# Splitting the first load of b by contraction slice in a GELU matmul chain

## The chip, the cores and the metric

The kernel runs on one core of one Trainium2 chip. The metric is the device time of one execution in microseconds (us), as the median of several runs. Engines are named as the profile names them: PE is TensorE (matmuls; PEld its weight loads), DVE is VectorE, ACT is ScalarE, POOL is GpSimd, SP is SyncE, which here only issues DMAs.

## What is computed

```python
# a: 1024 x 1024, b: 1024 x 2048, c: 2048 x 1024, all float32
h = a @ b
h = gelu_tanh(h)          # 0.5*h*(1 + tanh(sqrt(2/pi)*(h + 0.044715*h**3)))
out = (h @ c).astype(float32)   # 1024 x 1024
```

## The kernel before

The whole order of work is written out by hand (`tc.manual_schedule()`, line 33): each engine runs its instructions in the order of the source, and waits between engines are made from the tiles that they write and read. The matmuls take bfloat16 operands in the first stage and mixed ones later.

**The main body.** The first product is made transposed: tile `hT[h]` holds gelu of a block of 128 columns of `b` by 512 rows of `a`. Columns 0 to 511 of `b` are multiplied plainly (`mm1`, line 112, by `block`, line 156), in eight contraction slices of 128 rows each (k = 0 to 7) and two halves of `a`'s rows (h = 0, 1). The other columns of `b`, and after them the second product with `c`, go through `seven` (line 306), a scheme with seven block products in place of eight (sums of blocks on DVE, products on PE, line 212). Stores of the result are issued by SP as the second product's blocks come out (`done2`, line 431, and `store`, line 428).

**The start, which the change touches.** `a` comes with rows on the partitions and has to be turned, so its path is: DMA to `sta` (float32), cast to bfloat16 `ab` (`cast_a`, line 128, the copies themselves at lines 108 for ACT and 110 for DVE), transposes on PE through a PSUM tile `pt` (`turn`, line 138, the transposes at line 145), copy to `aT` on DVE (line 146). `b` needs only a cast from `stb` to `b1` (`cast_b`, line 149).

SP issues five loads, lines 75 to 79, one behind the other on one queue:

| line | what it loads | size | read by |
|---|---|---|---|
| 75 | `a`, first 512 rows, columns 0 to 255, to `sta` | 512 KB | `cast_a(0, 0)` on DVE |
| 76 | `b`, contraction slices 0 and 1, columns 0 to 511, to `stb[:, 0:2]` | 512 KB | `cast_b(0)` on DVE and ACT, `cast_b(1)` on ACT |
| 77 | `a`, last 512 rows, columns 0 to 255 | 512 KB | `cast_a(1, 0)` on DVE and ACT |
| 78 | `a`, first 512 rows, columns 256 to 511 | 512 KB | `cast_a(0, 1)` on ACT and DVE |
| 79 | `b`, slice 2, columns 0 to 511 | 256 KB | `cast_b(2)` on ACT |

All other loads are issued by POOL on its own queue and cast on the way (lines 85 to 104). POOL holds them back with one small copy, `gate` (line 81), that waits for line 75's data.

Until the first data is there, PE runs filler matmuls on a constant (`stir`, line 122, recorded at line 125). The order around the first matmuls is, on all engines together:

```python
stir(256, 256, 256, 256, 256)
tn = turn(0, 0, 4, cast_a(0, 0, nc.vector))
next(tn)                                     # 4 transposes, copy to aT (slice 0)
stir(128)
cast_b(0, nc.vector, nc.vector, nc.scalar)   # 128 + 128 columns on DVE, 256 on ACT
next(tn)                                     # 4 transposes, copy to aT (slice 1)
stir(64)
cast_b(1, nc.scalar)                         # 512 columns on ACT
ab = cast_a(1, 0, nc.vector, nc.scalar)      # needs line 77's data
block(0, range(4), (0,))                     # 4 matmuls of slice 0
block(0, range(2), (1,))                     # 2 matmuls of slice 1
for _ in turn(1, 0, (7, 6), ab):             # 8 transposes of line 77's data
    pass
```

**The stores.** SP's queue has eight completion semaphores, which its transfers take in turn; a transfer waits, when it is issued, for the one eight places before it. Before the change SP issues 5 loads and 19 stores, 24 in all. In `done2` the blocks (i, l) = (0, 0) with j = 1 and j = 2 are stored in two halves each, as the first results of the second product; the ones that follow are stored whole, up to the last two, which are halves again (line 376).

Of the kernel before, what the change touches and what calls it, by code (L numbers as in the profile page):

```python
# [19 lines left out]
def kernel(ctx, tc, a, b, c, out):  # L20
    nc = tc.nc
# [3 lines left out]
    H = 512  # L25
# [4 lines left out]
    bv = b.rearrange("(kt p) n -> p kt n", p=128)  # L30
# [9 lines left out]
    def slot(tag, shape, dt, name):  # L40
        return big.tile(shape, dt, name=name, tag=tag)
# [4 lines left out]
    def pieces(tag, bufs, shape, dt, name):  # L46
        return small.tile(shape, dt, name=name, tag=tag, bufs=bufs)
# [17 lines left out]
    stb = slot("x0", [128, KT, H], F32, "stb")  # L65
# [3 lines left out]
    def a_part(h, q):  # L69
        return av[:, 4 * h:4 * h + 4, ds(q * 256, 256)]  # L70

    def b_part(q):
        return bv[:, 2 * q:2 * q + 2, 0:H]

    nc.sync.dma_start(out=sta[:, 0, 0], in_=a_part(0, 0))  # L75
    nc.sync.dma_start(out=stb[:, 0:2], in_=b_part(0))  # L76
    nc.sync.dma_start(out=sta[:, 1, 0], in_=a_part(1, 0))
    nc.sync.dma_start(out=sta[:, 0, 1], in_=a_part(0, 1))
    nc.sync.dma_start(out=stb[:, 2], in_=bv[:, 2, 0:H])
# [19 lines left out]
    for n in range(2):  # L99
        for k in range(0, KT, 4):  # L100
            nc.gpsimd.dma_start(out=b2[:, k:k + 4, ts(n, H)],
                                in_=bv[:, k:k + 4, ds(1024 + n * H, H)])
# [151 lines left out]
    for q in range(1, 3):  # L254
        k = 2 * q
# [172 lines left out]
    def store(mt, q0, w, ot, eng=None):  # L428
        (eng or nc.sync).dma_start(out=out[ts(mt, 128), ds(q0, w)], in_=ot)

    def done2(i, l, j, p):
        if (i, l) == (1, 0):
            ot = pieces("o", 4, [128, H], F32, "ot")
            nc.vector.tensor_copy(ot, p)
            p = ot
        n = 2 if (i, l) == (0, 0) and j else 1
        for q in range(n):
            r = ds(q * (H // n), H // n)
            store(4 * i + j, l * H + q * (H // n), H // n, p[:, r])

    def between2(n):
# [12 lines left out]
        elif n == "P73":  # L454
            two.t4(two.t[1], 4)

    seven(two, done2, between2)


# [28 lines left out]
```

## Time and profile before

| | us |
|---|---|
| median of 3 runs (117.45 to 117.9) | 117.73 |
| span of the profiled execution, first to last instruction | 115.7 |
| median less span | 2.0 |
| PE busy in that span | 111.1 (96%) |
| DVE busy | 90.0 (78%) |
| ACT busy | 51.4 (44%) |
| granted TensorE clock, mean | 1.00 |

The profiled execution has no time of its own beside its span; the table sets the span against the median of the timed runs. All times below count from the first instruction of the profiled execution. An engine's busy time is the union of its instructions; TensorE's instructions overlap each other, so that a matmul of 512 columns is recorded with 0.379 us while matmuls in a row start every 0.216 us. "Landing" is the time at which the last of a DMA's completion events arrived; each of the 16 DMA engines sends one.

The chain of work that ended last is PE for 90% of the span and DMA for 5%. 21 MB are read from HBM; the DMA engines are busy until about 54 us, after that only with stores.

### The profile page before, as it was taken

To read this page: it belongs to the slowest core of one execution; us is meant where nothing else is said; L and a number is where in the kernel's file an instruction comes from. 1 tells how busy PE (TensorE), PEld (TensorE's weight loads), DVE (VectorE), ACT (ScalarE), POOL (GpSimd) and SP (SyncE) were. 2 spreads that over 40 slices of the span, in tenths; PEclk is the share of its full clock that TensorE was granted. 3 is DMA by queue.
4 is the path that set the end of the run, shared out by engine and by line. 5 is a ranking of instruction groups with operands and counts; after the bars stand their busy time and mean duration, and the time that the engine had idled before them with its cause. 6 is when DMAs were issued, how large, how long until landed. Compare 5 with 4: busy or idle time off the path is not lost.

```text
span 115.7 us, 1461 instructions
## 1 busy us (share of the span) xinstructions
PE 111.1 (96%) x542; PEld 77.1 (67%) x542; DVE 90.0 (78%) x107; ACT 51.4 (44%) x86; POOL 17.2 (15%) x29
## 2 busy tenths in 40 slices
PE   7989999999999999999999999999999999999980
PEld 6645555546776447888885444688888888888860
DVE  0347748789999998935699999999999986954770
ACT  5053000999259997166698429500124982000000
POOL 2497755223322000000000000000000000000000
PEclk9999999999999999999999999999999999999999
DMA  2999999999999999998000000060000002014993
GB/s 69 295 381 229 200 199 205 204 208 205 206 211 209 212 213 209 212 210 168 8 0 0 6 0 0 38 235 0 0 0 0 0 4 91 1 73 176 370 363 106
DMA packets 13414, 15.94 MB, mean 138 GB/s; under 512 B 736, under 2 KB 9312, under 8 KB 13408
## 3 DMA queue, kind: packets, MB, share of 16 engines
q0 software_dynamic: 8672, 9.31, 47.6%
q1 hardware_dynamic: 4736, 6.56, 15.8%
q8 instruction: 4, 0.07, 0.3%
q14 instruction: 2, 0.02, 0.0%
HBM read 20.97 MB, written 4.19 MB: 218 GB/s over the span
## 4 chain that ended last, share of the span: by engine, by line
PE 90%; DMA 5%; SPq 1%; DVE 1%; issue 0%
PE ps L212 76%; PE ps L114 11%; DMA sta<-in_a_dram 5%; PE pt L145 3%; SPq L76 0%; DVE ab L110 0%; SPq L75 0%; DVE ot L375 0%
## 5 line engine op out<-in xcount | busy, mean ns | idle before, releaser
L212 PE MATMUL ps<-x,s 128*128 128x512 f32 x128 | 29.6, 391 | 0.0
L212 PEld LDWEIGHTS ps<-x,s 128*128 128x128 f32 x128 | 24.0, 188 | 5.1
L212 PE MATMUL ps<-x,x 128*128 128x512 f32 x96 | 22.9, 394 | 0.0
L212 PEld LDWEIGHTS ps<-x,x 128*128 128x128 f32 x96 | 18.0, 188 | 3.9
L114 PE MATMUL ps<-aT,b 128*128 128x512 bf16 x64 | 16.1, 379 | 0.2 <-DVE b L110 0.2
L298 ACT ACTIVATE v<-ps 128x512 f32<-128x512 f32 x10 | 6.0, 599 | 19.1 <-PE ps L212 19.1
L212 PE MATMUL ps<-c_sb,hT 128*128 128x512 bf16 (+1 forms) x72 | 14.2, 356 | 0.0
L212 PE MATMUL ps<-x 128*128 128x512 f32 x56 | 13.2, 392 | 0.0
L212 PEld LDWEIGHTS ps<-x 128*128 128x128 f32 x56 | 10.2, 188 | 2.6 <-ACT u L298 0.4
L118 ACT ACTIVATE hT<-ps 128x512 bf16<-128x512 f32 x14 | 7.3, 595 | 9.7 <-PE ps L114 9.7
L212 PEld LDWEIGHTS <-hT 128*128 128x128 bf16 x72 | 6.9, 98 | 7.0 <-issue 0.5
L118 ACT ACTIVATE hT<-ot 128x512 bf16<-128x512 f32 x18 | 10.4, 624 | 2.0 <-DVE ot L303 2.0
L212 PE MATMUL ps<-aT,b 128*128 128x512 bf16 x48 | 10.7, 379 | 0.0
L146 DVE COPY aT<-pt 128x512 bf16<-128x512 bf16 x16 | 6.7, 423 | 5.1 <-PE pt L145 5.1
L303 DVE TENSOR_TENSOR ot<-ps,u 128x512 f32<-128x512 f32 x10 | 6.7, 690 | 5.1 <-ACT u L298 5.1
L303 DVE TENSOR_TENSOR ot<-ps,v 128x512 f32<-128x512 f32 x10 | 6.7, 688 | 4.8 <-DMA out_dram<-ot 3.8
L170 DVE TENSOR_TENSOR x<-c_sb 128x1024 fp32r<-128x1024 bf16 x8 | 9.3, 1226 | 0.0
L114 PEld LDWEIGHTS <-b 128*128 128x128 bf16 x64 | 5.7, 98 | 4.5 <-DVE b L110 0.3
L212 PEld LDWEIGHTS <-b 128*128 128x128 bf16 x48 | 4.6, 98 | 5.7 <-issue 0.3
L104 POOL DMA_DIRECT2D c_sb<-in_c_dram x8 | 5.6, 702 | 13.1 <-DMA b<-in_b_dram 12.4
L170 DVE TENSOR_TENSOR x<-b 128x1024 fp32r<-128x1024 bf16 (+1 forms) x4 | 7.0, 1752 | 0.6 <-issue 0.6
L298 ACT ACTIVATE u<-ps 128x512 f32<-128x512 f32 x10 | 5.9, 598 | 3.4 <-PE ps L212 3.2
(44 smaller groups left out, 111.3 us busy)
## 6 DMA issues: line engine op xcount, KB each, us to landing
c_sb<-in_c_dram POOLq DMA_DIRECT2D x8, 512.0 KB, 20.0
out_dram<-ot SPq DMA_DIRECT2D x13, 256.0 KB, 2.1
b<-in_b_dram POOLq DMA_DIRECT2D x6, 512.0 KB, 15.3
sta<-in_a_dram SPq DMA_DIRECT2D x3, 512.0 KB, 6.1
abq<-in_a_dram POOLq DMA_DIRECT2D x5, 256.0 KB, 7.9
out_dram<-ot SPq DMA_DIRECT2D x6, 128.0 KB, 2.0
stb<-in_b_dram SPq DMA_DIRECT2D x1, 512.0 KB, 5.3
b<-in_b_dram POOLq DMA_DIRECT2D x2, 256.0 KB, 8.2
```

Source lines behind the costliest of these rows:

```text
L104: nc.gpsimd.dma_start(out=c_sb[:, t:t + 2], in_=cv[:, t:t + 2])
L114: nc.tensor.matmul(p, b1[:, k, ts(t, 128)], aT[:, h, k], start=(k == 0), stop=(k == KT - 1))
L118: nc.scalar.activation(hT[h][:, t], p, AF.Gelu_apprx_tanh)
L145: nc.tensor.transpose(pt[:, n, ts(m, 128)], ab[:, m, ts(n, 128)], ident)
L146: nc.vector.tensor_copy(aT[:, h, 2 * q + n], pt[:, n])
L170: nc.vector.tensor_tensor(out=dst[:, r], in0=x[:, r], in1=y[:, r], op=op)
L212: nc.tensor.matmul(p[:, ds(c0, w)], l[:, k, ts(j, 128)], r[:, k, ds(c0, w)], start=(start and k == 0), stop=(k == self.kt - 1), skip_group ...
L298: nc.scalar.activation(st, p, AF.Copy)
L303: nc.vector.tensor_tensor(out=ot, in0=p, in1=st, op=ADD)
```

## The change

SP's second load becomes two loads, one for each contraction slice, of 256 KB each, at the same place in the order. In return the second of the two early blocks that were stored in halves, j = 2, is stored whole, so that SP's transfers are 24 as before (6 loads, 18 stores). All numbers of source lines behind the first hunk grow by one. The order of the computing instructions on PE, DVE, ACT and POOL stays the same; `cast_b(0)` now waits for the first of the two loads and `cast_b(1)` for the second.

```diff
@@ -73,7 +73,8 @@
     nc.sync.dma_start(out=sta[:, 0, 0], in_=a_part(0, 0))
-    nc.sync.dma_start(out=stb[:, 0:2], in_=b_part(0))
+    for k in range(2):
+        nc.sync.dma_start(out=stb[:, k], in_=bv[:, k, 0:H])
     nc.sync.dma_start(out=sta[:, 1, 0], in_=a_part(1, 0))
     nc.sync.dma_start(out=sta[:, 0, 1], in_=a_part(0, 1))
     nc.sync.dma_start(out=stb[:, 2], in_=bv[:, 2, 0:H])
@@ -433,7 +434,7 @@
-        n = 2 if (i, l) == (0, 0) and j else 1
+        n = 2 if (i, l, j) == (0, 0, 1) else 1
```

## The prediction

> **What bounds the kernel now.** I read the table of busy time first: TensorE (PE) is busy 111.1 of 115.7 us, so only a stretch in which PE stands still can pay. Then the chain of work that ended last, in order of time, to find where PE does stand still:
>
> ```profile
> 0.74 0.44 SPq L75
> 1.18 0.05 issue
> 1.24 0.50 SPq L76
> 1.73 0.05 issue
> 1.78 6.10 DMA sta<-in_a_dram
> 7.88 0.02 issue
> 7.90 0.44 DVE ab L110
> 8.34 0.05 issue
> 8.38 0.62 PE pt L145 x8
> ...
> 24.46 87.96 PE ps L212 x400
> 112.42 0.02 issue
> 112.44 0.42 DVE ot L375
> ```
>
> The columns are start, length and what ran. The program is one PE chain from 8.38 us to the end (every piece left out here is PE, too), and its start is set by the DMA of line 77, the second part of a. That load is issued third, behind the load that the change splits. So whatever the change does to the first matmuls, the end moves only if line 77's data moves, or if PE is late by itself at 8.38. The timeline of that corner, engine by engine:
>
> ```profile
> 1.24 0.50 SPq L76 DMA_DIRECT2D stb<-in_b_dram  x1
> 1.78 0.46 SPq L77 DMA_DIRECT2D sta<-in_a_dram  x1
> 5.58 0.42 DVE L146 COPY aT<-pt 128x512 bf16<-128x512 bf16 x1 [0.49 <-PE pt L145]
> 6.54 0.94 ACT L108 ACTIVATE b<-stb 128x256 bf16<-128x256 f32 x2 [4.30 <-DMA stb<-in_b_dram]
> 6.54 0.36 DVE L110 CAST b<-stb 128x128 bf16<-128x128 f32 x2 [0.53 <-DMA stb<-in_b_dram]
> 6.83 1.47 PE L114 MATMUL ps<-aT,b 128*128 128x512 bf16 x6 [0.15 <-DVE b L110]
> 7.90 0.43 DVE L110 CAST ab<-sta 128x512 bf16<-128x512 f32 x1 [0.67 <-DMA sta<-in_a_dram]
> 8.38 0.62 PE L145 MATMUL pt<-ident,ab 128*128 128x128 bf16 x8
> ```
>
> Brackets hold the idle time and what ended it. The six first matmuls wait only 0.15 us for b's casts. They start every 0.216 us, the sixth at 7.92, so PE has streamed them by 8.13 and stands until 8.38: 0.25 us of idle that belongs to line 77's landing (7.88), not to b's.
>
> Last, the busy time of the DMA engines in stretches, to see why line 77 lands when it does (the last column is GB/s, the one before it the share of DMA engines busy):
>
> ```profile
> 3.00:3.60 0.60, 0.60 (x3) 0.46 (x2) 0.00 (x0) 0.00 (x0) 0.00 (x0) 1.00 1.05 369
> 4.20:4.70 0.50, 0.50 (x2) 0.38 (x2) 0.30 (x1) 0.00 (x0) 0.27 (x1) 1.00 0.87 274
> 4.70:5.60 0.90, 0.83 (x8) 0.45 (x7) 0.41 (x2) 0.00 (x0) 0.90 (x2) 1.00 0.97 256
> 6.20:8.30 2.10, 1.94 (x12) 0.91 (x10) 1.09 (x4) 1.33 (x3) 2.10 (x4) 1.00 1.09 378
> ```
>
> The engines are never idle from 3 us on: the five loads go through one after another, so line 77 waits for bytes in front of it, not for its issue. The rows at 4.20 and 4.70 are b's load (the load to be split), and it is slow: 256 to 274 GB/s against 369 and 378 for a's loads around it. Semaphore events of the trace say the same: the loads' last arrivals are at 4.38 (a, line 75), 6.51 (b, line 76), 7.88 (line 77), 9.31 (line 78) and 9.96 (line 79), so 512 KB took 2.13 us for b and 1.37 and 1.43 us for a.
>
> **The change, part by part.**
>
> *Slice 0 of b lands earlier.* b's packets run from 3.59 to 6.13, in 16 per DMA engine; slice 0 is the first eight of them, if the queue keeps its order. Half of the 256 packets have started by about 4.8 us, the slower engines by 5.1; b's last packet started at 6.13 and the last arrival was 0.38 later, so slice 0 arrives at about 5.45 (estimate). What does that release? DVE's two casts come in DVE's order behind the copy that ends at 6.00, so they run at 6.01 to 6.37. PE is busy with transposes and two filler matmuls (line 125, starts 6.28 and 6.40, 0.11 us each) until about 6.51. So the first matmul starts at 6.51 instead of 6.83: 0.32 us earlier. ACT's cast of slice 0 (0.42 us) moves to about 5.5. Its next one waits for slice 1 at about 6.51, takes 0.61 and ends at 7.15; PE wants it after four matmuls, at 6.51 + 4 x 0.216 = 7.37, so this new wait, which holds ACT's cast of line 77's data behind it, costs nothing; it would from a landing at 6.75 on. The six matmuls are through at 6.51 + 6 x 0.216 = 7.81. And then PE waits for line 77: the 0.32 us turn into idle time, 0.57 instead of 0.25 us. Gain on the path: **0**.
>
> *One more issue on SP, ahead of lines 77 to 79.* A row: SP's five issues take 0.44 to 0.55 us each. The third load is issued at about 2.3 instead of 1.78, the last at about 3.4 instead of 2.83. Line 75's first packet ran at 1.85, 0.67 after its issue was over; so line 77's packets are ready by 2.3 + 0.5 + 0.7 = 3.5 us, and the engines come to them at 5.58. The 2.1 us of queue hide it, and likewise for lines 78 and 79 (ready by 4.6 at the latest, needed at 6.9 and 8.3). Cost 0; it would show if the loads in front shrank by over 2 us.
>
> *One more completion per DMA engine.* Completion packets take 9 ns in the records, and between lines 77 and 78 there is no gap in the packets at all (84 to 95 of them start in every 0.25 us from 6.25 to 8.5). +0.01 us on the path; nothing below, 0.05 above.
>
> *b's slow rate.* Here the trace can't say. Packets of b carry stalls: 0.49 us per engine over their usual 84 ns each, most of it between 4.75 and 5.6 us. Line 79, a single slice of b in the very form that the change uses, has none (128 packets at 84 ns). But a joint load of two slices on POOL's queue later (b's slices 4 and 5: 512 KB in 1.26 us) is not slow either, and line 75, the first of all, has 0.17 us of stalls. If the pairing of two rows 1 MiB apart makes the stalls, they go: down to a's pace, 2.13 - 1.40 = -0.73 us for line 77. If the stretch from 3.6 to 5.6 us is slow for another reason, nothing changes. If the start of a load makes them, a second start adds 0.17, up to b's own 0.49. I take 0, because the later joint load, the nearest row in form, isn't slow, so that time rather than form seems to decide; the ends -0.73 and +0.49 stay for the range. A gain is cut by PE: its matmuls end at 7.81, so at most 8.38 - 7.81 = 0.57 reaches the end.
>
> *What follows at once.* Line 78's data (9.31) is hardly early: ACT's cast of it ends at 9.84, PE loads it as weights at 9.89 and is free at 9.94. It moves with line 77 in the same queue, so one shift serves for both.
>
> The rule that speaks against the change is the Trainium skill's, "DMA: Bandwidth & Descriptors", section "Anatomy of one DMA": a DMA costs about 2.0 us plus its bytes at 436 GB/s, so small ones should be merged. Charged in full, a second DMA would add 2.0 us, for some 119.7 us. The trace disagrees where loads queue: line 79's 256 KB arrived 0.65 us after line 78's, with no 2 us between them.
>
> *The store.* Rows 256 to 383 of the output, left half, go out as one transfer instead of two: one issue of about 0.4 us less on SP at about 76 us. SP's next store is issued at 94.55, some 18 us later, and the buffer is reused no earlier, so nobody waits. The number of transfers on SP's queue stays 24, and with it each late store waits on the same predecessor as before. Cost 0; a stall would have to exceed that distance.
>
> Sum: 0 + 0 + 0.01 + 0 + 0 = **+0.01 us** on the profiled span of 115.7, so 115.7. The median of the three times, 117.73, lies 2.06 above that span; the change touches nothing of that rest. **Forecast 117.7 us.** A difference of under 0.5% (0.6 us) is about what a measurement of this kernel can't tell from no change.
>
> **Rivals.**
>
> *b's load speeds up (0.25).* For it: 256 to 274 GB/s, and no stall in line 79. Against: the later joint load at full speed. Line 77 lands 0.15 to 0.73 earlier, the end 0.15 to 0.57: 117.15 to 117.6, middle 117.4.
>
> *Slower: line 77 lands later (0.2).* One mechanism, in SP's queue between 4.6 and 6.5 us: slice 1 stalls as a new load's first packets did (0.17 us per engine in line 75), up to b's own 0.49. It decides from the first 0.05 us, as PE waits there with no slack. 117.9 to 118.2, at worst 118.3 with the completion's cost.
>
> *The change doesn't do what it says (0.15).* The two pieces' packets mix, or slice 0 also lands near 6.5: the first matmul stays at 6.8 and the time at 117.7.
>
> The forecast itself, slice 0 early and nothing gained, has 0.4.
>
> **How the numbers follow.** Forecast and third rival (0.55) are within 0.2 us of 117.7. The range takes the first rival down to its end, 117.15, and the second to 118.2. Faster by over 0.5% means below 117.14: the end of the first rival with the medians' own scatter (the three runs lie 0.45 apart), 0.12. Slower by over 0.5% means above 118.32: beyond the end of the second, with the same scatter, 0.11. The rest, 0.77, is within.
>
> **What would show it.** In the profile after: DVE's cast of b at about 6.0 and the first matmul of line 115 (114 before) at about 6.5; the wait of PE before the eight transposes grown to some 0.57 us; line 78 (77 before) landing within 0.1 us of 7.88; the PE chain still without a gap from there to the end. I am wrong if that landing moves by more than 0.1 either way, or if a wait appears in the chain that isn't there now.

## The result and the profile after

The changed kernel takes 118.58 us (median of 5 runs, 118.19 to 119.37) against 117.66 us before (6 runs, 117.45 to 118.04): a ratio of 1.0086, 95% interval 1.0062 to 1.0109. The forecast was 117.7, and the predicted range ended at 118.2. Runs over 1.5% above the fastest of the same kernel, here one at 121.85, are left out of the medians and ratios, here and below.

The chain of work that ended last, in order of time (start, length, what), in the profile after, which is of the fastest of these runs (118.19 us):

```profile
0.74 0.44 SPq L75
...
1.23 0.49 SPq L77
...
1.78 0.42 SPq L77
...
2.24 6.36 DMA sta<-in_a_dram
...
8.62 0.44 DVE ab L111
...
9.11 0.62 PE pt L146 x8
...
113.19 0.42 DVE ot L376
```

It is the old chain with one number changed. The load of a behind b (line 78 now, line 77 before) lands at 8.60 instead of 7.88; PE begins its eight transposes at 9.11 instead of 8.38. From there to DVE's last piece it takes 104.08 us, before 104.06. So the span's growth from 115.7 to 116.4 us is all in that one landing. The timeline of the corner (idle time and what ended it in brackets) shows the rest:

```profile
5.84 0.42 DVE L147 COPY aT<-pt 128x512 bf16<-128x512 bf16 x1 [0.72 <-PE pt L146]
6.19 0.39 DVE L111 CAST b<-stb 128x128 bf16<-128x128 f32 x2
6.19 0.42 ACT L109 ACTIVATE b<-stb 128x256 bf16<-128x256 f32 x1 [3.95 <-DMA stb<-in_b_dram]
6.77 1.46 PE L115 MATMUL ps<-aT,b 128*128 128x512 bf16 x6
6.86 0.63 ACT L109 ACTIVATE b<-stb 128x512 bf16<-128x512 f32 x1 [0.25 <-DMA stb<-in_b_dram]
8.62 0.43 DVE L111 CAST ab<-sta 128x512 bf16<-128x512 f32 x1 [1.45 <-DMA sta<-in_a_dram]
9.11 0.62 PE L146 MATMUL pt<-ident,ab 128*128 128x128 bf16 x8 [0.88 <-DVE ab L111]
```

Slice 0 did land ahead of slice 1, but at 6.16, only 0.35 before the whole load of before (6.51), and slice 1 at 6.83, 0.32 after it. The first matmul starts at 6.77 instead of 6.83; then PE stands for 0.88 us in front of the transposes. The DMA engines in the same stretches as in the prediction (last columns: share of DMA engines busy, GB/s):

```profile
3.00:3.60 0.60, 0.60 (x3) 0.47 (x2) 0.00 (x0) 0.00 (x0) 0.00 (x0) 1.00 1.09 387
4.20:4.70 0.50, 0.50 (x2) 0.37 (x2) 0.27 (x1) 0.00 (x0) 0.23 (x1) 1.00 0.93 143
4.70:5.60 0.90, 0.90 (x6) 0.42 (x5) 0.43 (x1) 0.00 (x0) 0.90 (x2) 1.00 0.98 245
6.20:8.30 2.10, 2.00 (x13) 0.93 (x11) 0.81 (x4) 1.03 (x2) 2.10 (x4) 1.00 1.02 352
```

The engines are as busy as before, and move less: 143 GB/s in the stretch at 4.20, where it was 274. In the records of the packets, the two slices carry 0.81 us of stalls per DMA engine (time over 84 ns for a packet of 2 KB), 0.59 of it in slice 0; the whole load of before had 0.49. And the engines come apart: the 16 arrivals of slice 0 lie between 4.47 and 6.16, those of the whole load before between 5.95 and 6.51.

### The profile page after: what moved, and what is told of

The parts are those of the page before. It is cut to its first block, busy times and chain, and to the rows that moved or that the text cites. A ratio compares the mean times of both kernels' runs of the same rounds, so it can differ in the third digit from the quotient of the medians.

```text
span 116.4 us, 1456 instructions
## 1 busy us (share of the span) xinstructions
PE 111.2 (96%) x536; PEld 77.5 (67%) x542; DVE 90.0 (77%) x107; ACT 51.5 (44%) x86; POOL 17.2 (15%) x29
## 3 DMA queue, kind: packets, MB, share of 16 engines
q0 software_dynamic: 8672, 9.31, 47.3%
## 4 chain that ended last, share of the span: by engine, by line
PE 89%; DMA 5%; SPq 1%; DVE 1%; issue 1%
PE ps L213 75%; PE ps L115 11%; DMA sta<-in_a_dram 5%; PE pt L146 3%; SPq L77 1%; DVE ab L111 0%; SPq L75 0%; DVE ot L376 0%
## 5 line engine op out<-in xcount | busy, mean ns | idle before, releaser
L115 PE MATMUL ps<-aT,b 128*128 128x512 bf16 x62 | 15.7, 379 | 0.1
L213 PE MATMUL ps<-aT,b 128*128 128x512 bf16 x46 | 10.6, 379 | 0.1
```

The costliest lines, as they stand in the source:

```text
L115: nc.tensor.matmul(p, b1[:, k, ts(t, 128)], aT[:, h, k], start=(k == 0), stop=(k == KT - 1))
L213: nc.tensor.matmul(p[:, ds(c0, w)], l[:, k, ts(j, 128)], r[:, k, ds(c0, w)], start=(start and k == 0), stop=(k == self.kt - 1), skip_group ...
```

## The experiments

My first theory (A): a single slice of b, read alone, stalls more than two in one load, and the load of a behind it lands when the slowest engine is through. Rivals: the store that isn't split any more (B), the number of transfers (C), any further load at the front of the queue (A2), a first contact with b's memory (D), the first microseconds of the program (E). In the ratios that follow, "before" is 117.53 to 117.58 us (medians of 11 to 28 runs).

**The load split alone, and the store alone.**

```diff
e1:  the new loads of b, and  n = 2 if (i, l) == (0, 0) and j else 1   (25 transfers)
e2:  the old load of b, and   n = 2 if (i, l, j) == (0, 0, 1) else 1   (23 transfers)
```

> Theory A (the split itself makes the first packets of b stall, so the load of a behind it lands later): as the changed kernel, 118.2 to 119.2 us, with that load of a landing near 8.6 us. Theory B (the store that is no longer split costs the time): 117.6 to 117.8. Theory C (the number of transfers matters): unlike both, since there are 25.

> Theory A: no change, 117.5 to 117.9 us. Theory B: 118.2 to 119.2.

The split alone: 119.28 us (median of 5 runs), ratio 1.0131 (1.0085 to 1.0177). The store alone: 117.58, ratio 1.0011 (0.9982 to 1.0040). So the cost is the split's and theory B falls. Whether the 25th transfer adds anything can't be told: the interval overlaps that of the whole change.

The profile of e2 holds a warning. It is of an execution of 118.22 us, 0.6 above that kernel's median. Its loads are those of the kernel before, and still b's whole load stalled by 0.86 us per engine, its arrivals lay 1.39 us apart, the load of a behind it landed at 8.55 us, and the end came when it came in the changed kernel's profile:

```profile
1.77 6.79 DMA sta<-in_a_dram
...
9.06 0.62 PE pt L145 x8
...
113.19 0.42 DVE ot L375
```

So this landing moves by 0.7 us from one execution to another even where b's load is whole. The two profiles above show what the end hangs on; how much of their 0.7 us, or of their stalls, is the split's, they can't show. For that there are the times of many runs, and the loads alone below.

**Another load split, b's whole.**

```diff
-    nc.sync.dma_start(out=sta[:, 1, 0], in_=a_part(1, 0))
+    for m in range(0, 4, 2):
+        nc.sync.dma_start(out=sta[:, 1, 0, m:m + 2], in_=av[:, 4 + m:6 + m, 0:256])
```

> The load of b is whole; the load of a behind it is split in two instead (rows in two halves). Theory A1 (what stalls is slice 0 of b read alone): 117.5 to 117.9 us. Theory A2 (every further load at the front of SP's queue costs a start): 118.2 to 119.2 us, with the second half of a landing 0.5 us late or more.

117.90 us, ratio 1.0029 (1.0006 to 1.0052), that is +0.3 us: at the upper end of what A1 had, and below A2. A further load costs something, but a third of what splitting b costs.

**b touched early.**

```diff
+    touch = consts.tile([128, 2, 16], F32, name="touch")
+    nc.scalar.dma_start(out=touch, in_=bv[:, 0:2, 0:16])
```

> The kernel before with one more tiny load: 64 bytes of each row of b's slices 0 and 1, issued by ACT at the very start, so that b is touched before its real load. Theory D (the stalls are a first contact with b's part of memory): the stalls of b's load (0.49 us per DMA engine) go, line 77 lands 0.4 to 0.7 us earlier and the time falls to 117.0 to 117.5 us. If they are not: no change or up to 0.3 us slower for the small packets, 117.6 to 118.0.

118.26 us, ratio 1.0060 (1.0036 to 1.0083), more than I had allowed for the small packets. b's load stalled as before (0.48 us per engine), and a's first load now landed at 4.75 instead of 4.38. Theory D falls.

**Loads alone.** To see the loads many times, two kernels that compute nothing issue SP's first loads twelve times over, in turns whole and in parts; for each load DVE copies one element that it brought, so that the start of a copy is the landing.

```python
whole:  a(0,0)  b[0:2]      a(1,0)  a(0,1)  b[2]
parts:  a(0,0)  b[0]  b[1]  a(1,0)  a(0,1)  b[2]
```

> A kernel of loads only (it computes nothing, and stores zeros): SP's first five or six loads, twelve times one after the other, in turns with b's load whole and in two parts, each turn begun when the one before has landed. Theory A (a slice of b read alone is slow in itself): in every turn with parts, the load of a behind b lands 0.5 to 1.2 us later after a's first than in the turns with b whole. Theory E (the loads stall only in the program's first 7 us, and the split only makes more of that): after the first turn both forms take the same, 2.8 us from a's first landing to its second within 0.1, and b's load takes 1.4 us, not 2.1.

> The same kernel of loads with the turns changed about, the form in parts first. Theory A: as before, every turn in parts is slower by 0.5 to 1.2 us. Theory E: only the first turn is slow, here the one in parts, by 0.5 us or more against a first turn with b whole. If the first turn is not slow in either kernel, the stalls need the other engines' work beside the loads.

The timeline of DVE in the first two turns of the first of these kernels (issued from 0.73 and from 10.19 us):

```profile
4.43 0.15 DVE L81 COPY mark<-sta 128x1 f32<-128x1 f32 x1 [4.43 <-DMA sta<-in_a_dram]
6.48 0.15 DVE L81 COPY mark<-stb 128x1 f32<-128x1 f32 x1 [1.90 <-DMA stb<-in_b_dram]
7.84 0.15 DVE L81 COPY mark<-sta 128x1 f32<-128x1 f32 x1 [1.21 <-DMA sta<-in_a_dram]
...
13.74 0.15 DVE L81 COPY mark<-sta 128x1 f32<-128x1 f32 x1 [3.58 <-DMA sta<-in_a_dram]
15.84 0.15 DVE L81 COPY mark<-stb 128x1 f32<-128x1 f32 x1 [1.94 <-DMA stb<-in_b_dram]
18.05 0.15 DVE L81 COPY mark<-stb 128x1 f32<-128x1 f32 x1 [2.05 <-DMA stb<-in_b_dram]
19.40 0.15 DVE L81 COPY mark<-sta 128x1 f32<-128x1 f32 x1 [1.20 <-DMA sta<-in_a_dram]
```

Whole, a's second load is there 3.41 us after a's first; in parts, 5.66, the slowest of the twelve turns in parts. Slice 0 alone, 256 KB, takes as long (2.10 us) as the two slices in one load (2.05). Over all turns of the two kernels, counted from a turn's first issue:

| 12 turns each | whole | in parts |
|---|---|---|
| a's second load lands, median (range), us | 7.18 (6.87 to 7.53) | 8.16 (7.48 to 9.19) |
| stalls of slices 0 and 1 per engine, median of the 11 turns whose packets are all on record, us | 0.56 | 0.77 |
| first to last arrival of the last of the two slices, median, us | 0.8 | 2.2 |

The first turns are like the later ones, and no engine computes beside them: theory E falls. A holds in the median, by 0.98 us, though not in every turn as I had said: the quickest turn in parts (7.48) came before the slowest whole one (7.53). Of the 0.98 us, the engines' mean stall gives 0.21, about a fifth; the rest goes with their coming apart, as a load has landed when its slowest engine is through.

**What a slice needs to stall.** The kernel before with lines 76 and 77 changed about:

> The kernel before with lines 76 and 77 changed about: b's whole load comes after the second load of a. If the stalls go with the time (3.5 to 6 us, whatever is loaded), a's second load now takes about 2.1 us and b's 1.4; if they go with b, a's takes 1.4 and b's 2.1. The program's time is worse by about 1 us either way, for the first matmuls wait for b longer.

a's second load took 1.6 us (4.24 to 5.82) and b's 3.3 (to 9.15): in this run the stalls go with b. The time was worse than I had said, 121.44 us in a single run; the last section returns to it. Then other forms of the loads alone:

> Loads only, four forms in turn, three times: b's slices 0 and 1 whole; in parts; in parts with slices 0 and 2 changed about (slice 2 comes where slice 0 came, slice 0 last); and whole rows of two slices in two column halves. Theory F (what stalls is a slice of b read right behind a's first load, with other loads queued behind it): in the changed-about form slice 2 stalls by 0.3 us per engine or more, and slice 0, last, not at all. Theory G (it is the address of slice 0): slice 0 stalls where it comes last, and slice 2 in front doesn't. The form in column halves: as whole, with a's second load at about 7.2 us after the first issue, if what counts is that two slices are read side by side; as in parts, 7.8 or later, if what counts is the number of loads.

The changed-about form in its first turn (issued from 21.98 us); the copies wait for a, slice 2, slice 1, a, a, slice 0 in this order:

```profile
25.53 0.15 DVE L81 COPY mark<-sta 128x1 f32<-128x1 f32 x1 [3.57 <-DMA sta<-in_a_dram]
27.68 0.15 DVE L81 COPY mark<-stb 128x1 f32<-128x1 f32 x1 [2.00 <-DMA stb<-in_b_dram]
29.38 0.15 DVE L81 COPY mark<-stb 128x1 f32<-128x1 f32 x1 [1.55 <-DMA stb<-in_b_dram]
30.73 0.15 DVE L81 COPY mark<-sta 128x1 f32<-128x1 f32 x1 [1.20 <-DMA sta<-in_a_dram]
32.13 0.15 DVE L81 COPY mark<-sta 128x1 f32<-128x1 f32 x1 [1.25 <-DMA sta<-in_a_dram]
32.77 0.34 DVE L81 COPY mark<-stb 128x1 f32<-128x1 f32 x4 [0.48 <-DMA stb<-in_b_dram]
```

Slice 2 in front takes 2.15 us, slice 0 at the end 0.64. So it is the place in the queue, not the address (F, not G); slice 2 stalled by 0.56, 0.92 and 0.19 us in the three turns (I had said 0.3 or more), slice 0 by nothing in any. The column halves decide nothing: a's second load at 7.19, 8.55 and 7.44, twice as with whole slices (6.96 to 7.55 here) and once as in parts (7.70 to 9.01). But they show that not every small load in front is slow. The first half, 256 KB of both slices right behind a's first load, took 0.67, 0.79 and 0.59 us, the second half 1.5 to 2.7. In the first of the three turns (copies for a's first load and the two halves):

```profile
36.81 0.15 DVE L81 COPY mark<-sta 128x1 f32<-128x1 f32 x1 [3.52 <-DMA sta<-in_a_dram]
37.48 0.15 DVE L81 COPY mark<-stb 128x1 f32<-128x1 f32 x1 [0.52 <-DMA stb<-in_b_dram]
38.99 0.15 DVE L81 COPY mark<-stb 128x1 f32<-128x1 f32 x1 [1.35 <-DMA stb<-in_b_dram]
```

> Loads only, four forms in turn, three times: b's slices 0 and 1 whole; slices 0, 1 and 2 in one load; slice 0, then a's second load, then slice 1; a's second load before slices 0 and 1 in parts. If a slice alone stalls wherever it is read early, the last two still stall in slice 0 (0.4 us per engine or more) and the last load of all lands later than with whole slices by 0.5 us or more. If three slices side by side stall less than two, the one load of 768 KB takes under 2.1 + 0.65 us.

Three slices in one load, 768 KB, land 2.1 us after a's first load, as two do (1.98 to 2.33 here), with 0.13 to 0.14 us of stalls in all. Single slices stall in slice 0 by 0.4 to 1.2 us wherever they are put early.

> Loads only, four forms in turn, four times: a's first load and slice 0 with nothing behind; a's first load and slices 0 and 1 in one load; a's first load and three single slices; slice 0 alone. Theory F1 (a slice stalls because other loads are queued behind it): in the first form slice 0 lands 0.65 to 0.8 us after a's first load, without stalls, and in the third form the first two slices stall and the last doesn't. Theory F2 (a slice stalls whenever it comes early, behind a's first load): it lands 1.5 us or more after it in the first form too, and the pair takes 2.1.

A turn of the form with three single slices, and one with slice 0 and nothing behind it:

```profile
34.10 0.15 DVE L81 COPY mark<-sta 128x1 f32<-128x1 f32 x1 [3.47 <-DMA sta<-in_a_dram]
35.65 0.15 DVE L81 COPY mark<-stb 128x1 f32<-128x1 f32 x1 [1.40 <-DMA stb<-in_b_dram]
36.35 0.15 DVE L81 COPY mark<-stb 128x1 f32<-128x1 f32 x1 [0.55 <-DMA stb<-in_b_dram]
36.99 0.21 DVE L81 COPY mark<-stb 128x1 f32<-128x1 f32 x2 [0.48 <-DMA stb<-in_b_dram]
...
43.74 0.15 DVE L81 COPY mark<-sta 128x1 f32<-128x1 f32 x1 [3.23 <-DMA sta<-in_a_dram]
44.49 0.21 DVE L81 COPY mark<-stb 128x1 f32<-128x1 f32 x2 [0.59 <-DMA stb<-in_b_dram]
```

The same slice behind the same load takes 1.55 us with two loads behind it and 0.75 with none (0.66 and 0.67 in two other turns, 1.55 in the very first). In three turns of four F1 has slice 0 right: the loads behind do it. It has slice 1 wrong: in the form with three single slices it took 0.61 to 0.70 us, at full pace. Two slices in one load with nothing behind took 1.3 to 2.0 us.

**In the kernel: one load of three slices, or three loads.** Same bytes, same order.

```diff
e7:  nc.sync.dma_start(out=stb[:, 0:3], in_=bv[:, 0:3, 0:H])
e8:  for k in range(3): nc.sync.dma_start(out=stb[:, k], in_=bv[:, k, 0:H])
     (both at line 76; line 79 gone)
```

> The kernel before with b's slices 0, 1 and 2 in one load at line 76 and line 79 gone (768 KB; 23 transfers). If more slices side by side stall less, as in the kernel of loads (768 KB in 2.1 us, as long as 512 KB), the load of a behind it still lands near 7.8 us or up to 0.2 earlier, and the time is 117.2 to 117.7 us. If the 256 KB more cost their own time, it lands 0.65 later: 118.1 to 118.4.

> The same bytes in the same order as the kernel with three slices in one load, but as three loads of one slice. Theory A (single slices stall): 1 us or more slower than that kernel, 118.7 to 120.5 us. If the form of the load doesn't matter, within 0.3 us of it.

One load: 117.97 us, ratio 1.0021 (0.9997 to 1.0044), between the two ranges that I had given. Three loads: 120.38 (median of 5 runs), ratio 1.0247 (1.0200 to 1.0295). The form alone is worth 2.4 us, which is theory A in the kernel itself. In the first, a's second load landed at 7.84 although 256 KB more ran ahead of it. No time was won, because the chain now waits for a load of POOL's queue, which a's first load gates: it lands at 16.36, where it landed at 15.84 before and PE didn't wait.

```profile
4.24 0.70 POOL gate L80
...
7.70 8.66 DMA abq<-in_a_dram
```

**Issue or queue?** Two accounts were left of why the loads behind matter: their issue on SP (H), or their standing in the queue (I).

> Loads only, four forms in turn, three times: four loads of a, then slices 0, 1 and 2 of b singly; four loads of a, then slices 0 and 1 whole and slice 2; a's first load, slice 0 and one load of a; and 512 KB of b as one slice of 1024 columns (rows of 4 KB) in the place of the two slices. Theory H (the issue of the following loads on SP, in the first 3.5 us, disturbs a slice that is read meanwhile): after four loads of a, with all issues over by 4.5 us and b read from about 8 us on, slice 0 doesn't stall and lands 0.65 to 0.8 us after a's fourth load. Theory I (what counts are the loads that stand in the queue behind a slice): slice 0 stalls there too, by 0.3 us per engine or more, and lands 1.2 us or more after a's fourth. With one load of a behind it, by H and I alike, slice 0 lands 1.0 us or more after a's first. One slice of 1024 columns: 2.1 us or more if one row per partition at a time is what stalls, 1.4 to 1.6 if the size of a partition's piece matters.

With four loads of a in front, in the first turn (from 0.73 us; the last issues on SP, then copies for a, a, a, a, slices 0, 1, 2):

```profile
2.86 1.62 SPq L88 DMA_DIRECT2D stb<-in_b_dram  x3
4.25 0.15 DVE L81 COPY mark<-sta 128x1 f32<-128x1 f32 x1 [4.25 <-DMA sta<-in_a_dram]
5.59 0.15 DVE L81 COPY mark<-sta 128x1 f32<-128x1 f32 x1 [1.19 <-DMA sta<-in_a_dram]
7.78 0.15 DVE L81 COPY mark<-sta 128x1 f32<-128x1 f32 x1 [2.04 <-DMA sta<-in_a_dram]
9.19 0.15 DVE L81 COPY mark<-sta 128x1 f32<-128x1 f32 x1 [1.26 <-DMA sta<-in_a_dram]
9.82 0.15 DVE L81 COPY mark<-stb 128x1 f32<-128x1 f32 x1 [0.47 <-DMA stb<-in_b_dram]
10.43 0.15 DVE L81 COPY mark<-stb 128x1 f32<-128x1 f32 x1 [0.46 <-DMA stb<-in_b_dram]
11.07 0.34 DVE L81 COPY mark<-stb 128x1 f32<-128x1 f32 x4 [0.48 <-DMA stb<-in_b_dram]
```

The slices, with others behind them, take 0.63 us each: I falls. But now a's third load is slow, 2.19 us instead of 1.35, and in all three turns (1.96 to 2.19); with b's slices 0 and 1 whole behind the four, it took 1.8 to 3.7. So a's loads aren't immune. And H doesn't explain this as it stands: SP's last issue was over at 4.48 us, and that load was read after it (the copies before and behind it stand at 5.59 and 7.78). 512 KB of b as one slice of 1024 columns took 2.1, 2.4 and 4.0 us, so a longer row is no cure. One load of a behind slice 0 is enough for 1.5 to 1.7 us. Last, H in the kernel, by issuing the two last loads later:

```diff
-    nc.sync.dma_start(out=sta[:, 0, 1], in_=a_part(0, 1))
-    nc.sync.dma_start(out=stb[:, 2], in_=bv[:, 2, 0:H])
     nc.gpsimd.tensor_copy(gate, sta[:, 0, 0, 3, 0:1])
+    nc.gpsimd.memset(sta[:, 0, 1, 0, 0:1], 0.0)
+    nc.sync.dma_start(out=sta[:, 0, 1], in_=a_part(0, 1))
+    nc.sync.dma_start(out=stb[:, 2], in_=bv[:, 2, 0:H])
```

> The kernel before, but SP issues lines 78 and 79 only when a's first load has landed and POOL has written one element (about 5.2 us instead of 2.3), so that just one load is issued behind b's while b is read. Theory H (issues of following loads disturb the load that is read): b's load stalls less and lands before 6.2 us, line 77 before 7.6; if the late issues don't then disturb line 77 in turn, the time is 117.0 to 117.5 us. If theory H is wrong: line 77 at 7.9 as before, and 117.5 to 118.2 us, for line 78 may come late.

> The changed kernel with the same delay of the issues of a's third load and b's slice 2. Theory H: two issues fewer while the two slices are read, so their stalls shrink and line 78 lands 0.4 us or more earlier than in the changed kernel (8.6 there); the time falls from 118.2 to 119.2 to 117.4 to 118.2 us. If theory H is wrong: as the changed kernel or slower, 118.2 to 119.5.

Both lost, by more than either theory had: 119.68 us (median of 4 runs; ratio 1.0181, 1.0165 to 1.0196) and 120.21 (4 runs; 1.0242, 1.0215 to 1.0268). The chain of the first:

```profile
4.33 0.70 POOL gate L79
5.03 0.04 POOL sta L80
...
5.09 6.10 DMA sta<-in_a_dram
```

The load issued at 5.09 lands at 11.19 instead of 9.31, for POOL's loads run beside it from 7.5 us on; before they began at 9.0, when SP's queue was nearly done. b's whole load landed at 6.50 and a's second at 8.38, not under 6.2 and 7.6; in parts they came at 7.24 and 8.58. So H's numbers were missed in the kernel, in a test that brought a second disturbance with it. The inner cause stays open.

## Why the prediction was wrong, point by point

**What bounds the kernel: right.** In the two profiles the landing of a's second load moved by 0.72 us and the span by 0.71; in e2's, landing and end moved together too (8.55 and 113.19).

**Slice 0 at 5.45 us: wrong, 6.16.** The estimate halved the whole load's time. Loads alone show that the first slice by itself takes about as long (1.5 to 2.3 us in the twelve turns) as both in one load (2.0 to 2.5). The copies therefore ran at 6.19, and the first matmul at 6.77, not 6.51. By itself that cost nothing, as PE waited for a's second load anyway.

**The further issue on SP, hidden by the queue: right as far as packets being late goes.** a's second load was issued by 2.67 us, and its first packets ran at 5.34 (5.58 before); it was not a late issue that moved it. What the issue may do to the load that is read meanwhile wasn't in the sum at all.

**The completion per engine, +0.01 us:** not to be seen beside the rest.

**b's slow rate, "I take 0": this step failed.** It measured +0.9 us in place of 0: the median time grew by 0.92, and in the loads alone a's second load lands 0.98 later. Bounds of -0.73 and +0.49 were set and 0 taken, because a later joint load on POOL's queue isn't slow and line 79, a single slice, has no stalls. Line 79 was read without its place: it is the last load of its queue and, as the changed-about form shows, slice 0 is as fast there. What the joint load on POOL's queue says of SP's was never tested. In front, single slices stall more. The upper bound was too low because it took an engine's mean stall for the delay of the landing: the mean grew by 0.21 us in the loads alone, well within the bound. Slices also drive the engines apart (first to last arrival 2.2 us, not 0.8), and the slowest one counts.

**The rule that merges small loads** had the sign right and not the size. The runs show 0.65 us for a single slice at the end of the queue, so no fixed cost of 2 us there, and about 1 us lost by splitting in front. The Trainium skill ("DMA: Bandwidth & Descriptors", "Anatomy of one DMA") gives its 2.0 us plus bytes at 436 GB/s as a fit for DMAs issued from GpSimd. The loads here are SP's, a condition that the prediction left out.

**The store at nothing: right** (ratio 1.0011, 0.9982 to 1.0040).

**The rivals.** The slower one was what happened, from a landing with no slack, but priced at 0.17 to 0.49 where 0.9 was due (1.5 to 1.7 for the split alone). It named slice 1 as the one that stalls; in the profile slice 0 has 0.59 of the 0.81 us. With 0.2 it also had too small a chance. The one that let b speed up had it the wrong way round.

## What to carry to other kernels

Splitting a load to get its first part earlier can be paid by the load behind it, as here, if that one is what the chain waits for: read whose landing starts the chain before asking whose landing comes first. A queue's rate is not a property of the shape of a load alone; a row for the same shape at the end of a queue is no price for it at the front. And a load lands with the slowest of its 16 engines, so that the spread of its arrivals belongs in the sum beside the mean. Last, one profile is one execution: the landing that this prediction turned on came at 7.88 us in one and 8.55 in another with the same loads.

## What the runs showed of the hardware

A load with others queued behind it can run at two thirds of its rate or less: a single slice of b, 256 KB, in 0.65 us at the end of the queue and, in three turns of four, with nothing behind, but in 1.5 to 2.6 us right behind a's first load; a's 512 KB in 1.35 or, third of four, in 1.8 to 2.2 (once 3.7). Not every one is slow: 256 KB as a column half of two slices took 0.59 to 0.79 us at the same place. More slices in one load make the stalls smaller: about 0.77, 0.56 and 0.13 us per engine for slices 0 and 1 singly, two slices and three slices in a load. Why is not settled.

PE's granted clock was 1.00 in nearly every stretch read here, but fell in one kernel that left PE idle for long. In the kernel with a's load in front PE was busy 0.97 of 3.3 us before b landed, and then ran 3.4 us at half the clock (the column behind the five engines):

```profile
6.80:10.10 3.30, 0.97 (x7) 0.57 (x6) 0.93 (x4) 0.93 (x3) 3.30 (x6) 1.00 1.08 295
10.20:13.50 3.30, 3.30 (x16) 1.72 (x15) 1.44 (x5) 1.56 (x4) 1.28 (x2) 0.50 1.36 206
13.60:17.00 3.40, 3.40 (x26) 1.84 (x25) 1.87 (x4) 0.00 (x0) 2.31 (x4) 1.00 1.40 198
```

The Trainium skill, "TensorE: Matmul & The Clock Gate", "Part 1: The HAM clock gate", says that the clock is set anew every 3.4 us by how busy the array was, and this run agrees. Half a clock over the 3.4 us is up to 1.7 us of matmul time (an estimate). It explains part of why that kernel took 121.44 us where I had said about 1 us more.
